# Layer 1's attention, two heads at a time: probabilities divided before they are turned, values as the stationary operand

## The chip, the cores and the metric

One core of a Trainium2 chip runs the whole program. The metric is device time in microseconds (us) of one execution, a median over runs; lower is better. A profile of one execution gives the start and the length of every instruction on the engines: TensorE (PE; its weight loads are listed as PEld), VectorE (DVE), ScalarE (ACT), GpSimd (POOL) and SyncE (SP), whose queue issues most DMAs.

## The reference, cut to what matters

A two-layer trunk over 256 frames of width 1024: retention and a dense feed-forward in layer 0, then shared keys and values, chunked attention and eight experts in layer 1. The change touches the attention alone. Each of 16 heads has 64 dimensions; a chunk of 64 frames attends to its own chunk and the eight before it, which with 256 frames means to all frames of its own and of earlier chunks.

```python
q = (xn @ w_q).reshape(B, nc, CHUNK, ATT_HEADS, ATT_HEAD_DIM) * (ATT_HEAD_DIM ** -0.5)
...
s = jnp.einsum('bihd,bjhd->bhij', q_c, k_band).astype(jnp.float32) + bias
s = jnp.where(valid, s, -jnp.inf)
a = jax.nn.softmax(s, axis=-1).astype(v_band.dtype)
return jnp.einsum('bhij,bjhd->bihd', a, v_band)
...
return o @ w_o
```

## The kernel before

Frames are two blocks of 128 (`tb` 0 and 1). Weights come from HBM as units of 1 MB through one queue (line 135, SP) into a few buffers; each unit is split into a high part (a cast on ScalarE, line 157) and the rest (a subtraction on VectorE, line 158), and a weight product is three matmuls with these parts. A buffer is free for the next load when its last subtraction is done.

Before the stage that the change touches, queries and keys are projected so that they lie turned: `qT` and `kT` hold 64 dimensions of the even head of a pair on partitions 0 to 63 and of the odd head on 64 to 127, with the 256 frames along the free axis. `vsb` holds the values with frames on the partitions. The first half of the heads is projected ahead of the loop. The second half's 8 rounds of 24 matmuls (lines 400 to 402, tile `kqps`) fill the first 8 rounds of the attention loop (`fill`). From the ninth round on the fill is the output projection, `out1(ch, tb)`: six matmuls of 512 columns each (lines 414, 415 and 418, tile `y`) for a chunk of 128 attended columns (two heads) and one block of frames.

A round `n` of the loop does, for one head each:

- `score(n)`: two f32 matmuls with 64 rows (lines 946 and 947, tile `sc`): the second block's queries against 256 keys, the first block's against 128. Then on VectorE the bias is added (950, 951), two maxima are taken (955, 956) and negated (957), and on ScalarE two exponentials (960, 963) also write the sums of their rows. After the odd head of a pair one reciprocal of four sums follows (967).
- `turn(n - 2)`: three transposes of 128 x 128 (974, tile `at`) and a copy out of PSUM on ScalarE (977).
- `values(n - 3)`: three f32 matmuls with the turned probabilities stationary, 128 columns, and 64 columns of values streaming (987 to 989, tile `ao`). After the odd head four scalings by the reciprocals write `dst` (996).
- `att_oT`, every second round: two transposes of a chunk of `dst` (1042, tile `otr`), split into high part and rest for the output projection (363, 364).

An f32 matmul of the program appears in the trace as two loads and two matmuls. In the loop the scheduler sets the order of every engine's work; after it an order written out by hand begins (`order`), which the last output chunks follow. PSUM has a ring of four banks (`bank`) for all of these tiles. The bias of a pair of heads is loaded by two DMAs (891, 892) into one of two buffers after the last add that reads the buffer.

The constants sit in one tile `cst` (loaded in two parts, lines 308 and 315); the exponent -0.5 of the norms, `nhalf`, has a tile of its own, set on line 316 and read on GpSimd.

Of the kernel before, what the change touches and what calls it, by code (L numbers as in the profile page):

```python
# [9 lines left out]
F32 = mybir.dt.float32  # L10
# [77 lines left out]
E_X, E_Y, E_END = 0, 8, 64  # L88
# [130 lines left out]
def trunk(ctx: ExitStack, tc: tile.TileContext, a, out):  # L219
# [15 lines left out]
    cst = base.tile([P, C_TILE], F32, name="cst")[:, :C_DEC]  # L235
    ext = base.tile([P, E_END], F32, name="ext")
    ones = base.tile([P, P], F32, name="ones")
    nhalf = base.tile([P, LINE], F32, name="nhalf")[:, :1]
# [642 lines left out]
    ap3 = r3.enter_context(tc.tile_pool(name="att3", bufs=3))  # L881
    vsb = ap_.tile([P, 2, D], F32, name="vsb")
# [54 lines left out]
    class Att:  # L937
# [3 lines left out]
        def score(self, hd):  # L941
            half, ch, par = hd // 8, (hd % 8) // 2, hd % 2
            rr = slice(par * 64, par * 64 + 64)
            q, k = qT[half][rr, ch, :], kT[half][rr, ch, :]
            b = bank("sc")
            nc.tensor.matmul(b[:, :T], q[:, P:], k, start=True, stop=True)
            nc.tensor.matmul(b[:, T : T + P], q[:, :P], k[:, :P], start=True, stop=True)
            bt = bias[(hd // 2) % 2][:, par, :]
            s = ap3.tile([P, T + P], F32, name="s")
            nc.vector.tensor_tensor(s[:, :T], b[:, :T], bt, op=OP.add)  # L950
            nc.vector.tensor_tensor(s[:, T:], b[:, T : T + P], bt[:, P:], op=OP.add)
            if par == 1 and hd // 2 + 2 < 8:
                load_bias(hd // 2 + 2)
            nm = s1("nm", 2)
            nc.vector.tensor_reduce(nm[:, 0:1], s[:, T:], axis=AX.X, op=OP.max)
            nc.vector.tensor_reduce(nm[:, 1:2], s[:, :T], axis=AX.X, op=OP.max)
            nc.vector.tensor_scalar(nm, nm, -1.0, None, op0=OP.mult)
            if par == 0:
                self.sum = s1("esum", 4)
            nc.scalar.activation(  # L960
                s[:, :T], s[:, :T], AF.Exp, bias=nm[:, 1:2], accum_out=self.sum[:, 2 + par : 3 + par]
            )
            nc.scalar.activation(s[:, T:], s[:, T:], AF.Exp, bias=nm[:, 0:1], accum_out=self.sum[:, par : par + 1])
            self.s[hd] = s
            if par == 1:
                rs = s1("rsum", 4)
                nc.vector.reciprocal(rs, self.sum)
                self.e[hd // 2] = rs
# [11 lines left out]
        def values(self, hd, dst):  # L980
            par = hd % 2
            t = self.t.pop(hd)
            if par == 0:
                self.o = bank("ao")
            o = self.o[:, :T].rearrange("p (b d) -> p b d", b=4)
            d = slice(hd * 64, hd * 64 + 64)
            nc.tensor.matmul(o[:, par, :], t[:, T:], vsb[:, 0, d], start=True, stop=True)
            nc.tensor.matmul(o[:, 2 + par, :], t[:, :P], vsb[:, 0, d], start=True, stop=False)
            nc.tensor.matmul(o[:, 2 + par, :], t[:, P:T], vsb[:, 1, d], start=False, stop=True)
            if par == 1:  # L990
                rs = self.e.pop(hd // 2)
                ch = (hd % 8) // 2
                for tb in range(2):
                    for j in range(2):
                        c = ch * P + j * 64
                        nc.vector.tensor_scalar(
                            dst[tb][:, c : c + 64], o[:, 2 * tb + j, :], rs[:, 2 * tb + j : 2 * tb + j + 1], None, op0=OP.mult
                        )
# [28 lines left out]
    dst, xo, wo, swapped, late = [], [], {}, [], []  # L1027
# [6 lines left out]

    def att_oT(ch):

        if ch % 2 == 0:
            xo.append(take_ht())
        b = bank("otr")[:, :T].rearrange("p (b t) -> p b t", b=2)
        c = ch % 4 * P  # L1040
        for tb in range(2):
            nc.tensor.transpose(b[:, tb, :], dst[ch // 4][tb][:, c : c + P], ident)
        f = slice(ch % 2 * 2, ch % 2 * 2 + 2)
        with hp(H1):
            split_bank(xo[-1][0][:, f, :], xo[-1][1][:, f, :], b)
# [14 lines left out]
    for n in range(19):  # L1060
        if n < 16:
            att.score(n)
        if n < 8:
            next(fill, None)
        if n == 8:
            for _ in fill:
                pass
            if not RE:
                st.retire(pairs1)
            elif not st.retired:  # L1070
                swap_right()
        for _ in range(PC if n % PM == 0 else 0):
            if late:
                st.raws.append(late.pop(0))
                st.load()
        if n >= 8 and n < 19 and outs[n - 8]:
            out1(*outs[n - 8])
        if 2 <= n <= 17:
            att.turn(n - 2)
        if n >= 3:  # L1080
            if (n - 3) % 8 == 0:
                dst.append([t512("ao0"), t512("ao1")])
            att.values(n - 3, dst[-1])
        if n >= 5 and n % 2:
            att_oT((n - 5) // 2)
    for x in OV[OO][1]:
        out1(*x)
    att_oT(7)
# [600 lines left out]
```

## Time and profile before

| | us |
|---|---|
| median of the runs shown | 1562.42 (1562.37 to 1562.57) |
| the profiled execution | 1563.2 |
| its span, first to last instruction | 1561.3 |
| busy: TensorE / weight loads / VectorE / ScalarE / GpSimd | 1537.8 / 1290.6 / 1275.3 / 1091.5 / 48.4 |

Busy time is the union of an engine's instructions. Matmuls overlap each other in flight: of two that follow each other, the first is still listed as running when the second starts. What a matmul costs TensorE is therefore the time from its start to the next one's start, not its listed length. The same holds, to a lesser degree, of VectorE and ScalarE. In a timeline neighbouring instructions of one kind are merged into a row (x2, x3), whose length runs from the first start to the last end.

### The profile page before, as it was taken

The numbers are of one execution on the slowest core, as the hardware profiler recorded it, in microseconds if no ns is written. First come the engines' busy times: TensorE is split into PE (matmuls) and PEld (weight loads), VectorE is DVE, ScalarE is ACT, GpSimd is POOL, SyncE is SP. The second block draws the span as 40 slices with busy tenths as digits, with TensorE's granted clock in tenths as the row PEclk, the third lists the DMA queues.
The fourth block names the chain that finished last, engine by engine and source line by source line (L and its number), as shares of the span: only waits on it lengthen the run. The fifth ranks groups of instructions, "written<-read, shape, count | busy, mean of one in ns | idle before, by whom it ended". The sixth has DMA issues, their size and how long they took to land.

```text
span 1561.3 us, 20789 instructions
## 1 busy us (share of the span) xinstructions
PE 1537.8 (98%) x7556; PEld 1290.6 (83%) x7556; DVE 1275.3 (82%) x1617; ACT 1091.5 (70%) x1461; POOL 48.4 (3%) x67
## 2 busy tenths in 40 slices
PE   7999999999999999999999999999999999999997
PEld 5888888888889888888888888888888888888886
DVE  7866675555774779999999999999999999999995
ACT  6545454554754658888878888888888788788774
POOL 1000010000000001000000000000000000000000
PEclk9999999999999999999999999999999999999999
DMA  8854476555463779999999999999999999999850
GB/s 294 286 180 167 162 254 216 187 188 196 149 217 124 267 269 378 412 391 381 378 382 394 381 373 388 366 382 390 373 386 391 375 368 398 380 369 390 310 211 30
DMA packets 206303, 473.56 MB, mean 303 GB/s; under 512 B 9168, under 2 KB 21328, under 8 KB 206192
## 3 DMA queue, kind: packets, MB, share of 16 engines
q1 hardware_dynamic: 202064, 457.87, 79.8%
q0 software_dynamic: 3840, 13.76, 2.4%
q8 instruction: 61, 1.00, 0.2%
q10 hardware_dynamic: 288, 0.52, 0.1%
q14 instruction: 50, 0.41, 0.1%
HBM read 462.16 MB, written 9.96 MB: 302 GB/s over the span
## 4 chain that ended last, share of the span: by engine, by line
PE 98%; ACT 1%; DVE 0%; DMA 0%; issue 0%; SPq 0%; POOL 0%; ACTq 0%; POOLq 0%; DVEq 0%
PE y L414 9%; PE y L415 9%; PE y L418 9%; PE g L333 8%; PE g L334 8%; PE g L335 8%; PE u L333 8%; PE u L335 8%; PE u L334 8%; PE vps L335 1%; PE vps L333 1%; PE vps L334 1%; PE htr L1230 1%; PE kqps L400 1%; PE qkps L401 1%; PE qkps L402 1%
## 5 line engine op out<-in xcount | busy, mean ns | idle before, releaser
L158 DVE TENSOR_TENSOR wlo<-raw,whi 128x512 fp32r<-128x512 f32 (+1 forms) x414 | 375.0, 929 | 109.5 <-ACT whi L157 94.4
L157 ACT CAST whi<-raw 128x512 fp32r<-128x512 f32 (+1 forms) x414 | 329.0, 812 | 139.0 <-PE y L418 49.7
L158 DVE TENSOR_TENSOR wlo<-more,whi 128x1024 fp32r<-128x1024 f32 (+1 forms) x275 | 327.4, 1214 | 26.4 <-ACT whi L157 14.1
L157 ACT CAST whi<-more 128x1024 fp32r<-128x1024 f32 (+1 forms) x275 | 284.6, 1049 | 58.6 <-PE y L418 29.5
L414 PE MATMUL y<-whi,ht 128*128 128x512 f32 x548 | 216.0, 394 | 0.5 <-ACT ht L363 0.5
L415 PE MATMUL y<-wlo,ht 128*128 128x512 f32 x548 | 213.9, 390 | 0.0
L333 PE MATMUL u<-whi,xd 128*128 128x512 f32 x448 | 180.3, 402 | 0.0
L333 PE MATMUL g<-whi,xd 128*128 128x512 f32 x456 | 177.9, 390 | 0.2 <-ACT xd L363 0.2
L335 PE MATMUL g<-whi,xd 128*128 128x512 f32 x456 | 177.9, 390 | 0.0
L334 PE MATMUL g<-wlo,xd 128*128 128x512 f32 x456 | 177.5, 389 | 0.0
L335 PE MATMUL u<-whi,xd 128*128 128x512 f32 x448 | 175.2, 391 | 0.0
L334 PE MATMUL u<-wlo,xd 128*128 128x512 f32 x448 | 174.5, 389 | 0.0
L418 PE MATMUL y<-whi,ht 128*128 128x512 f32 x548 | 169.0, 390 | 0.0
L414 PEld LDWEIGHTS y<-whi,ht 128*128 128x128 f32 x548 | 102.9, 188 | 21.9 <-ACT ht L363 1.0
L418 PEld LDWEIGHTS y<-whi,ht 128*128 128x128 f32 x548 | 102.9, 188 | 21.8
L415 PEld LDWEIGHTS y<-wlo,ht 128*128 128x128 f32 x548 | 103.0, 188 | 20.8
L158 DVE TENSOR_TENSOR wlo<-mraw,whi 128x1024 fp32r<-128x1024 f32 x91 | 109.3, 1223 | 10.3 <-ACT whi L157 5.1
L157 ACT CAST whi<-mraw 128x1024 fp32r<-128x1024 f32 x91 | 94.7, 1056 | 19.1 <-PE y L418 9.5
L158 DVE TENSOR_TENSOR wlo<-spare,whi 128x1024 fp32r<-128x1024 f32 x84 | 100.6, 1221 | 8.1 <-ACT whi L157 4.3
L335 PEld LDWEIGHTS g<-whi,xd 128*128 128x128 f32 x456 | 85.6, 188 | 18.2 <-DVE xd L364 0.4
L333 PEld LDWEIGHTS g<-whi,xd 128*128 128x128 f32 x456 | 85.6, 188 | 18.1 <-ACT xd L363 0.5
L157 ACT CAST whi<-spare 128x1024 fp32r<-128x1024 f32 x84 | 87.5, 1055 | 18.6 <-PE y L418 9.1
(363 smaller groups left out, 2632.0 us busy)
## 6 DMA issues: line engine op xcount, KB each, us to landing
more<-in_w_gate_moe_dram SPq DMA_DIRECT2D x56, 1024.0 KB, 7.1
more<-in_w_down_moe_dram SPq DMA_DIRECT2D x46, 1024.0 KB, 7.7
raw<-in_w_up_moe_dram SPq DMA_DIRECT2D x45, 1024.0 KB, 7.0
more<-in_w_up_moe_dram SPq DMA_DIRECT2D x35, 1024.0 KB, 7.0
raw<-in_w_gate_moe_dram SPq DMA_DIRECT2D x25, 1024.0 KB, 7.2
raw<-in_w_in_a_dram SPq DMA_DIRECT2D x23, 1024.0 KB, 5.2
raw<-in_w_down_moe_dram SPq DMA_DIRECT2D x22, 1024.0 KB, 7.3
mraw<-in_w_down_moe_dram SPq DMA_DIRECT2D x22, 1024.0 KB, 7.1
```

What stands on the lines that cost most here:

```text
L157: self.nc.scalar.copy(hi[:, f], r[:, g])
L158: (lo_engine or self.nc.vector).tensor_tensor(lo[:, f], r[:, g], hi[:, f].bitcast(F32), op=OP.subtract)
L333: nc.tensor.matmul(o, lh, rh, start=start, stop=False)
L334: nc.tensor.matmul(o, lh, rl, start=False, stop=False)
L335: nc.tensor.matmul(o, ll, rh, start=False, stop=stop)
L400: nc.tensor.matmul(o, wh[:, c, f], xh_, start=k == 0, stop=False)
L401: nc.tensor.matmul(o, wh[:, c, f], xl_, start=False, stop=False)
L402: nc.tensor.matmul(o, wl[:, c, f], xh_, start=False, stop=k == KC - 1)
L414: nc.tensor.matmul(ys[nb], xs[0][:, k, :], wh[:, c, f], start=first and k == 0, stop=False)
L415: nc.tensor.matmul(ys[nb], xs[0][:, k, :], wl[:, c, f], start=False, stop=False)
L418: nc.tensor.matmul(ys[nb], xs[1][:, k, :], wh[:, c, f], start=False, stop=last and k == n - 1)
L1230: nc.tensor.transpose(b[:, c, :m], x[:m, c0 + c * P : c0 + (c + 1) * P], ident[:m, :m])
```

## The change

Scores are computed for two heads at once, as four neighbouring matmuls: even and odd head for 256 keys, then both for 128. After the exponentials each head takes its own reciprocal of two sums, and two scalings divide the probabilities in place, ahead of the turn. `values(pr)` has the values of a head stationary (64 columns) and the turned probabilities streaming (256 columns, then 128). The even head's result lands on partitions 0 to 63 of a bank, the odd head's on 64 to 127, frames along the free axis. That is the turned chunk that the output projection reads, so `att_oT` goes: the bank is split at once. The layout of `s` is reversed (first block first). The loop runs over nine pairs of rounds instead of 19 rounds, and TensorE's order in it is the order in which it is written; `between(n)` is the projection or output round that was `fill` or `out1` before. `s` has four buffers of its own, and `nhalf` becomes a column of the constants' tile.

```diff
-E_X, E_Y, E_END = 0, 8, 64
+E_X, E_Y, E_END = 0, 8, 16
...
-    cst = base.tile([P, C_TILE], F32, name="cst")[:, :C_DEC]
+    cst_all = base.tile([P, C_TILE], F32, name="cst")
+    cst, nhalf = cst_all[:, :C_DEC], cst_all[:, C_DEC : C_DEC + 1]
...
-    nhalf = base.tile([P, LINE], F32, name="nhalf")[:, :1]
...
+    ap4 = r3.enter_context(tc.tile_pool(name="att4", bufs=4))
...
-        def score(self, hd):
...
+        def scores(self, pr):
+
+            half, ch = pr // 4, pr % 4
+            rows2 = [slice(par * 64, par * 64 + 64) for par in range(2)]
+            qk = [(qT[half][rr, ch, :], kT[half][rr, ch, :]) for rr in rows2]
+            bs = [bank("sc") for _ in range(2)]
+            for b, (q, k) in zip(bs, qk):
+                nc.tensor.matmul(b[:, P : P + T], q[:, P:], k, start=True, stop=True)
+            for b, (q, k) in zip(bs, qk):
+                nc.tensor.matmul(b[:, :P], q[:, :P], k[:, :P], start=True, stop=True)
+            for par in range(2):
+                self.exps(2 * pr + par, bs[par])
+
+        def exps(self, hd, b):
...
+            s = ap4.tile([P, T + P], F32, name="s")
...
+            sums = s1("esum", 2)
+            nc.scalar.activation(s[:, P:], s[:, P:], AF.Exp, bias=nm[:, 1:2], accum_out=sums[:, 1:2])
+            nc.scalar.activation(s[:, :P], s[:, :P], AF.Exp, bias=nm[:, 0:1], accum_out=sums[:, 0:1])
+            nc.vector.reciprocal(sums, sums)
+            nc.vector.tensor_scalar(s[:, P:], s[:, P:], sums[:, 1:2], None, op0=OP.mult)
+            nc.vector.tensor_scalar(s[:, :P], s[:, :P], sums[:, 0:1], None, op0=OP.mult)
             self.s[hd] = s
...
-        def values(self, hd, dst):
...
+        def values(self, pr):
+
+            b = bank("ao")
+            two = [(b[j * 64 : j * 64 + 64], self.t.pop(2 * pr + j), slice((2 * pr + j) * 64, (2 * pr + j) * 64 + 64)) for j in range(2)]
+            for o, t, d in two:
+                nc.tensor.matmul(o[:, :T], vsb[:, 0, d], t[:, :T], start=True, stop=False)
+            for o, t, d in two:
+                nc.tensor.matmul(o[:, P:T], vsb[:, 1, d], t[:, T:], start=False, stop=True)
+            if pr % 2 == 0:
+                xo.append(take_ht())
+            f = slice(pr % 2 * 2, pr % 2 * 2 + 2)
+            with hp(H1):
+                split_bank(xo[-1][0][:, f, :], xo[-1][1][:, f, :], b[:, :T].rearrange("p (b t) -> p b t", b=2))
...
-    def att_oT(ch):
...
+    by_pairs = tc.manual_schedule(engines={mybir.EngineType.PE})
+    by_pairs.__enter__()
+
+    def between(n):
         if n < 8:
             next(fill, None)
+        elif outs[n - 8]:
+            out1(*outs[n - 8])
+
+    for m in range(9):
+        if m < 8:
+            att.scores(m)
+        if m == 4:
             for _ in fill:
                 pass
...
+        if late:
+            st.raws.append(late.pop(0))
+            st.load()
+        between(2 * m)
+        if m:
+            att.turn(2 * m - 2)
+            att.turn(2 * m - 1)
+        between(2 * m + 1)
+        if m:
+            att.values(m - 1)
+    by_pairs.__exit__(None, None, None)
     for x in OV[OO][1]:
         out1(*x)
-    att_oT(7)
```

## Rows read from the trace of the kernel before

**Rows 1.** The page: busy time of the engines, and TensorE's tenths in 40 slices

```profile
PE 1537.8 (98%) x7556; PEld 1290.6 (83%) x7556; DVE 1275.3 (82%) x1617; ACT 1091.5 (70%) x1461; POOL 48.4 (3%) x67
...
PE   7999999999999999999999999999999999999997
```

**Rows 2.** Busy by stretch: PE, PEld, DVE, ACT, POOL; then granted clock, DMA share, GB/s

```profile
477.25:549.96 72.71, 72.26 (x483) 63.67 (x482) 44.60 (x152) 40.72 (x116) 0.00 (x0) 1.00 0.55 193
...
600.00:700.00 100.00, 100.00 (x465) 82.90 (x464) 93.30 (x95) 80.52 (x86) 3.19 (x4) 1.00 1.04 402
```

**Rows 3.** Waits of the load queue, 560 to 1540: total us, times, longest

```profile
SPq L135 <- DVE wlo L158: 776.5, 324, 12.0
```

**Rows 4.** Timeline (start, length) of TensorE at 459: projection steps

```profile
459.68 0.28 PE L401 MATMUL kqps<-xt,phi 128*128 128x256 f32 x1
459.80 0.28 PE L402 MATMUL kqps<-xt,plo 128*128 128x256 f32 x1
```

**Rows 5.** Timeline around the score block of head 8, TensorE and its weight loads

```profile
513.90 0.47 PE L414 MATMUL y<-whi,ht 128*128 128x512 f32 x1
514.30 0.70 PE L946 MATMUL sc<-kT,qT 64*128 64x256 f32 x2
514.62 0.40 PEld L947 LDWEIGHTS sc<-kT,qT 64*128 64x128 f32 x2
514.84 0.38 PE L947 MATMUL sc<-kT,qT 64*128 64x128 f32 x2
515.15 0.50 PE L415 MATMUL y<-wlo,ht 128*128 128x512 f32 x1
515.49 0.40 PE L414 MATMUL y<-whi,ht 128*128 128x512 f32 x1
...
516.43 0.49 PE L974 MATMUL at<-cst,s 128*128 128x128 f32 x3
516.76 0.33 PE L987 MATMUL ao<-vsb,at 128*128 128x64 f32 x2
```

**Rows 6.** Groups by line, 477.25 to 549.96: busy us, mean ns, idle before

```profile
L158 DVE TENSOR_TENSOR wlo<-raw,whi 128x512 fp32r<-128x512 f32 x24 | 15.8, 687 | 3.8 <-ACT whi L157 3.8
...
L996 DVE TENSOR_SCALAR ao<-ao,rsum 128x64 f32<-128x64 f32 x32 | 7.2, 278 | 10.3 <-PE ao L989 10.3
...
L364 DVE TENSOR_TENSOR ht<-otr,ht 128x256 fp32r<-128x256 f32 x8 | 3.4, 421 | 3.4 <-ACT ht L363 3.3
...
L363 ACT CAST ht<-otr 128x256 fp32r<-128x256 f32 x8 | 3.0, 374 | 2.9 <-PE otr L1042 2.9
```

**Rows 7.** One line's instructions: a scaling of 256 columns, min/median/max ns

```profile
L476 DVE TENSOR_SCALAR ang<-ang,cst x1: 354/354/354, 23.5 to 23.5; 128x256 f32<-128x256 f32 x1
```

**Rows 8.** Timelines of VectorE and ScalarE, 524.8 to 527.5: one head's chain

```profile
524.80 0.16 DVE L957 TENSOR_SCALAR nm<-nm 128x2 f32<-128x2 f32 x1
...
525.73 0.42 DVE L950 TENSOR_TENSOR s<-sc,bias 128x256 f32<-128x256 f32 x1 [0.20 <-PE sc L947]
...
526.60 0.28 DVE L955 TENSOR_REDUCE nm<-s 128x1 f32<-128x128 f32 x1
...
525.00 0.51 ACT L960 ACTIVATE s<-s,nm 128x256 f32<-128x256 f32 x1 [0.48 <-DVE nm L957]
...
525.80 0.19 ACT L963 ACTIVATION_READ_ACCUMULATOR s<-s,nm 128x1 f32 x1
527.47 0.48 ACT L977 COPY at<-at 128x384 f32<-128x384 f32 x1 [1.49 <-PE at L974]
```

**Rows 9.** DMA issues from 476 to 550: count, KB each, median us to landing

```profile
bias<-in_bias_hi_dram SPq DMA_DIRECT2D x6, 128.0 KB, 3.1
```

**Rows 10.** The constants' tile, 0 to 24: its readers, its loads, their time to landing

```profile
L369 PE MATMUL xtr<-cst,xh x16: 421/421/476, 10.1 to 17.9; 128*128 128x128 f32 x16
...
L315 SPq DMA_DIRECT2D cst<-in_cst_dram x1: 1098/1098/1098, 4.1 to 4.1; - x1
...
DMA to landing us min/median/max: 1.9/5.5/9.2
```

More of the change, by code (lines that the diff above doesn't have):

```diff
@@ L939, in __init__ @@
             self.s, self.e, self.t = {}, {}, {}
-        def score(self, hd):
[L942 to L947, printed above, removed]
+        def scores(self, pr):
[10 more added lines that the diff above has]
+        def exps(self, hd, b):
+            par = hd % 2
             bt = bias[(hd // 2) % 2][:, par, :]
-            s = ap3.tile([P, T + P], F32, name="s")
-            nc.vector.tensor_tensor(s[:, :T], b[:, :T], bt, op=OP.add)
-            nc.vector.tensor_tensor(s[:, T:], b[:, T : T + P], bt[:, P:], op=OP.add)
+            s = ap4.tile([P, T + P], F32, name="s")
+            nc.vector.tensor_tensor(s[:, P:], b[:, P : P + T], bt, op=OP.add)
+            nc.vector.tensor_tensor(s[:, :P], b[:, :P], bt[:, P:], op=OP.add)
             if par == 1 and hd // 2 + 2 < 8:
@@ L954, in score @@
             nm = s1("nm", 2)
-            nc.vector.tensor_reduce(nm[:, 0:1], s[:, T:], axis=AX.X, op=OP.max)
-            nc.vector.tensor_reduce(nm[:, 1:2], s[:, :T], axis=AX.X, op=OP.max)
+            nc.vector.tensor_reduce(nm[:, 0:1], s[:, :P], axis=AX.X, op=OP.max)
+            nc.vector.tensor_reduce(nm[:, 1:2], s[:, P:], axis=AX.X, op=OP.max)
             nc.vector.tensor_scalar(nm, nm, -1.0, None, op0=OP.mult)
[L958 to L963, printed above, removed]
+            sums = s1("esum", 2)
[4 more added lines that the diff above has]
+            nc.vector.tensor_scalar(s[:, :P], s[:, :P], sums[:, 0:1], None, op0=OP.mult)
             self.s[hd] = s
[L965 to L968, printed above, removed]
         def turn(self, hd):
@@ L978, in turn @@
             self.t[hd] = t
-        def values(self, hd, dst):
[L981 to L998, printed above, removed]
+        def values(self, pr):
[10 more added lines that the diff above has]
+                split_bank(xo[-1][0][:, f, :], xo[-1][1][:, f, :], b[:, :T].rearrange("p (b t) -> p b t", b=2))
     att = Att()
@@ L1026, in trunk @@
     y = new_y()
-    dst, xo, wo, swapped, late = [], [], {}, [], []
+    xo, wo, swapped, late = [], {}, [], []
     def swap_right():
@@ L1033, in swap_right @@
         swapped.append(True)
-    def att_oT(ch):
[L1037 to L1045, printed above, removed]
     def out1(ch, tb, n=99):
@@ L1059, in trunk @@
     outs = [(0, 0), (0, 1), (1, 0), (1, 1), (2, 0), (2, 1), (3, 0), (3, 1)] + OV[OO][0]
-    for n in range(19):
-        if n < 16:
-            att.score(n)
+    by_pairs = tc.manual_schedule(engines={mybir.EngineType.PE})
+    by_pairs.__enter__()
+    def between(n):
         if n < 8:
             next(fill, None)
-        if n == 8:
+        elif outs[n - 8]:
[4 more added lines that the diff above has]
+        if m == 4:
             for _ in fill:
                 pass
-            if not RE:
-                st.retire(pairs1)
-            elif not st.retired:
+            if not st.retired:
                 swap_right()
[L1072 to L1085, printed above, removed]
+        if late:
[9 more added lines that the diff above has]
+    by_pairs.__exit__(None, None, None)
     for x in OV[OO][1]:
         out1(*x)
-    att_oT(7)
     order = tc.manual_schedule(engines=eng)
```

## The prediction, made before the result was known

> **What bounds the kernel now.** I read the page's busy line and its slices first: TensorE is busy 98% of the span, and no slice but the first and the last is under 9 tenths [rows 1]. That alone proves little, since the ends of matmuls are modelled; so I looked at the stretch that the change touches, from the first score matmul to the first output matmul of the last chunk, 477.25 to 549.96, 72.7 us. There TensorE is covered for 72.26 us at a granted clock of 1.00 (the 2.4 GHz level), VectorE for 44.60 and ScalarE for 40.72 [rows 2]; the 0.45 us left open is the wait for the last turned chunk. So in this stage the time is the sum of the steps from one matmul's start to the next one's, and the change is worth the difference of two such sums. The other engines matter only if they come to keep TensorE waiting.
>
> Is a gain kept afterwards? In the experts TensorE is covered 100.00 of 100 us [rows 2], while the queue of weight loads waits for free buffers (776.5 us in 324 waits from 560 to 1540) [rows 3]. TensorE sets the pace there too, and the loads are ahead of it. A stage that ends 10 us earlier starts the experts 10 us earlier; I keep the whole gain.
>
> **The parts of the stage.** What stays: 192 projection matmuls of 256 columns (eight rounds of 24) at 0.12 us from start to start [rows 4], 23.0 us; 66 output matmuls of 512 columns (eleven rounds of six) at 0.235 (four steps from 515.49 to 516.43 [rows 5]), 15.5 us; 48 turns at 0.109 (0.33 for three [rows 5]), 5.2 us. Together 43.7 us. The other 72.7 - 43.7 = 29.0 us are scores, values, 16 transposes of attended rows, and the edges between kinds of work.
>
> One score block shows the edges [rows 5]. The output matmul ahead of it starts at 513.90 and the block at 514.30: 0.40 where 0.235 is usual, so 0.17 is a wait for the array to empty. The second pass starts with the load at 514.62 and takes until 514.84, 0.215; the first took 0.32, so 0.107 of it is a weight load that nothing hides. The four passes (each f32 matmul is two) are 2 x 0.215 + 2 x 0.108 = 0.645; the block ends at 515.15, 0.85 after its start, so 0.094 more is a wait behind it. The matmul after that takes 0.34: another 0.107 of unhidden load. Entering a 64-row block costs 0.28, leaving it 0.20.
>
> **Scores.** Two heads now stand side by side, one on partitions 0 to 63, one on 64 to 127. Nothing in the trace has two neighbouring matmuls on opposite halves, so I bound it. One after the other, a pair is 2 x 0.645 = 1.29; wholly side by side it is 0.645. The two passes of a head share their rows and must follow each other, and the order is A, A, B, B, then the shorter A, A, B, B, started in order. Then A's second pass runs beside B's first, B's second beside the short A's first, and so on: 0.215 x 3 + 0.108 x 2 = 0.86. I take that, an estimate between the ends: only the order stands in the way, not the rows.
>
> **Values.** Now 64 columns of values stand still, and 256, then 128, columns of turned probabilities stream. That is as many columns as in the scores, so the prices of a pair are the same: 0.86, between 0.645 and 1.29. (Before, the six passes of a head were followed after some 0.6 to 0.7 us.) The new blocks get edges that the old ones, 128 wide, did not have; I price them as the score block's.
>
> **Edges.** In the written order there are 10 entries from 128-wide work (two scores, eight values), 10 exits to it, and 6 places where values are followed at once by scores: 10 x 0.28 + 10 x 0.20 + 6 x 0.20 = 6.0 us.
>
> **Transposes of attended rows** are gone, 16 x 0.11 = 1.8 us, with the 0.45 us wait at the end: the last values are now followed by a whole round of output (1.4 us), which hides one cast and one subtraction (0.37 and 0.42 [rows 6]).
>
> **Sum.** 29.0 us becomes 8 x 0.86 + 8 x 0.86 + 6.0 = 19.8, a gain of 9.2. With everything wholly side by side it is 12.7, with everything one after the other 2.4.
>
> **VectorE and ScalarE.** Out go 32 scalings (0.278 us [rows 6]) and 8 reciprocals; in come 16 reciprocals and 32 larger scalings, for which the nearest row is 0.354 us (256 columns, a scalar per partition) [rows 7]. That is some 3 us more VectorE work, beside 28 us of slack [rows 2]: nothing on the path. But it lies in the chain from scores to turns. For a pair: adds and maxima 1.15 us a head and a negation 0.16, twice, 2.6; exponentials of the second head 1.0; reciprocal and two scalings 0.8; some 4.5 us with the hand-overs [rows 7, 8]. Its cover in the second half of the loop is three output rounds (4.2), two turns (0.65), a values and a score block (2.4): 7.2 us. Two subtractions of weights and one of a chunk (0.69, 0.69, 0.42 [rows 6]) may stand between: 6.3. It fits, barely.
>
> Less sure is the copy of turned probabilities. It had a whole head's round until its use; now it has one output round, 1.4 us, in the second half. Two copies of 0.48 fit, but the next pair's exponentials (1.0 a head) come to ScalarE at the same time [rows 8]. Behind none of them the values wait 0, behind one head's 0.75 us: over the four such rounds 0 to 3.0 us, and nothing in the first half, where a round is 2.9 us. I take 1.2. What is queued behind such a wait is all of TensorE's work, since its order is now written out.
>
> The moved bias loads (two DMAs a pair, 3.1 us to land [rows 9]) are issued after the second head's adds and wanted two rounds, over 12 us, later: nothing, and 3 us a round if they stood behind a blocked weight load in their queue. The norms' constant moves into the tile of the large constants, whose second load, issued at 4.1, takes up to 9.2 to land; the transposes at 10.1 already read that tile's first columns before then [rows 10], so columns are told apart: nothing, or some 5 us at the start if they were not.
>
> The Trainium skill, "TensorEngine Tiling (Array Packing)", section "Key Properties", says that changing the tiling mode drains TensorE; that speaks against this change, which makes a second tiled block of the values. The rows' 0.17 and 0.094 bear a drain out for rows; none shows one for columns. Were the values free of it, the edges would be those of eight score blocks, 8 x 0.48 = 3.8 us, and the gain 11.4; by the rule it stays 9.2.
>
> **Rivals.** (a) *Nothing runs side by side.* Only edges and transposes are saved: 2.4 less 1.2 of waiting, 1561.2 us. For it: no row shows two matmuls streaming at once. Against it: a score matmul uses 64 rows and costs what its columns cost, so the other half is idle. (b) *Only scores overlap,* or only values: 9.2 - 8 x 0.43 - 1.2 = 4.6, 1557.8. (c) *Slower: each change of half is an edge.* A block of a pair changes halves three times, 48 times in 16 blocks. At the 0.20 of leaving and reloading that is 9.6 us on top of (a), 1570.8 us; the loss passes 3.1 us from 4.3 / 48 = 0.09 us a change. For it: the trace has no change without other work between. Against it: within a block a load runs ahead during the pass before it. (d) *Slower: the divided probabilities come late,* and the written order holds all of TensorE for them. Past 7.2 us of chain each us is paid in five rounds; at 9.7 it is 12.5 us against 9.2, 1565.7. For it: 6.3 of 7.2 are used. (e) *Wholly side by side:* 12.7 less 1.2, 1550.9. Against it: a head's two passes share their rows.
>
> Of (e), the Trainium skill, "TensorE: Matmul & The Clock Gate", section "Measured speedup vs the span model", says that a packed group lasts about one matmul plus 4 ns a tile. By it the time would be that of (e); no run here shows it, and it does not speak of two-pass f32 matmuls.
>
> **How the numbers follow.** The profiled execution took 1563.2 us (span 1561.3); less 9.2, plus 1.2, that is 1555.2. The median of the runs shown, 1562.42, is 0.8 lower, so I forecast 1554.4. Chances: forecast 0.60, (a) 0.13, (b) 0.11, (c) 0.06, (d) 0.05, (e) 0.05. The range, 1549.7 (12.7 gained, no waiting) to 1563.0 (2.4 gained, 3.0 of waits), leaves out (c) and (d). A difference under 0.2%, 3.1 us, can't be told from none: faster is the forecast, (b) and (e), nearly all of it, 0.75; same is most of (a), 0.14; slower 0.11.
>
> **What would show it.** Right: score passes of opposite halves that start under 0.1 us apart; a pair's score block and values block near 1.06 us each with the first load and the wait behind; under 2 us of waits of TensorE in the stage; a stage near 65 us. Wrong: blocks of 1.5 us (a), gaps at each change of half (c), TensorE waiting for VectorE ahead of turns (d), or for the copies by more than 3 us. A later stage that gives the gain back would upset the second paragraph.

## The result, and the profile after

| us | before | after |
|---|---|---|
| median of the runs compared | 1562.49 (1562.37 to 1562.90) | 1549.49 (1549.08 to 1549.70) |
| the profiled execution, and its span | 1563.2, 1561.3 | 1549.7, 1547.9 |
| the stage, first score matmul to first output matmul of the last chunk | 72.68 | 59.40 |
| the rest, from there to the end of the span | 1011.37 | 1011.28 |

After takes 0.9917 of the time of before (95% interval 0.9905 to 0.9929): 13.0 us faster. The forecast was 1554.4, and the range ended 0.2 us above the measured time, at 1549.7. That miss is smaller than the spread of after's own runs (0.6 us); the distance to the forecast, 4.9 us, is not, and it is what has to be explained. The stage shrank by 13.28 us, and what follows took as long as ever (1011.07 to 1011.45 in every kernel below). The stage begins between 476.0 and 477.6 us, up to 1.6 us apart in these kernels, so below the length of the stage says more than the median.

The page and the windows of after, to lay beside [rows 1, 2]: TensorE is still the engine that is hardly ever idle, also in the stage.

```profile
PE 1524.8 (99%) x7508; PEld 1276.6 (82%) x7508; DVE 1277.0 (82%) x1625; ACT 1090.1 (70%) x1461; POOL 48.2 (3%) x67
...
PE   7999999999999999999999999999999999999997
```
```profile
477.24:536.64 59.40, 59.24 (x435) 49.81 (x435) 46.95 (x160) 39.24 (x116) 0.00 (x0) 1.00 0.61 216
...
600.00:700.00 100.00, 100.00 (x465) 82.94 (x464) 93.01 (x96) 81.06 (x89) 1.60 (x3) 1.00 1.03 398
```

Within the stage TensorE is covered 59.24 of 59.40 us, VectorE 46.95, ScalarE 39.24. The waits of the load queue from 560 to 1540 are those of [rows 3], one fewer:

```profile
SPq L135 <- DVE wlo L158: 775.8, 323, 11.9
```

Now the blocks. The timeline of TensorE in after, around the scores of pair 5 (start, length, merged rows), to lay beside [rows 5]:

```profile
514.24 0.70 PE L949 MATMUL sc<-kT,qT 64*128 64x256 f32 x4
514.77 0.39 PE L951 MATMUL sc<-kT,qT 64*128 64x128 f32 x4
515.09 0.50 PE L414 MATMUL y<-whi,ht 128*128 128x512 f32 x1
```

The first row lasts 0.70 us, as that of [rows 5] did, but holds four passes, not two. The block ends 0.85 after its start, as one head's did. Two heads cost what one did. That the passes of the two heads start together, a narrow stretch shows (514.05 to 514.245; the x2 are one pass of each head):

```profile
513.81 0.49 PE L993 MATMUL ao<-at,vsb 128*64 128x128 f32 x3
514.24 0.49 PE L949 MATMUL sc<-kT,qT 64*128 64x256 f32 x2
```

In the single records they start at 514.236 and 514.242, 0.006 us apart, and the other three couples of the block by 0.007. Pairs are counted from 0, and the round that computes the scores of pair 5 ends with the values of pair 4. These, in the same view:

```profile
518.25 0.62 PE L418 MATMUL y<-whi,ht 128*128 128x512 f32 x2
518.79 0.65 PE L991 MATMUL ao<-at,vsb 128*64 128x256 f32 x4
519.28 0.39 PE L993 MATMUL ao<-at,vsb 128*64 128x128 f32 x4
519.60 0.49 PE L949 MATMUL sc<-kT,qT 64*128 64x256 f32 x2
```

Eight passes in 0.80 us (518.79 to 519.60). Over the stage all eight score blocks take 0.85, seven of the eight values blocks 0.80 and one 1.01.

The groups by line of after in the stage, to lay beside [rows 6, 7]:

```profile
L158 DVE TENSOR_TENSOR wlo<-raw,whi 128x512 fp32r<-128x512 f32 x24 | 15.6, 683 | 1.2 <-ACT whi L157 1.1
...
L972 DVE TENSOR_SCALAR s<-s,esum 128x256 f32<-128x256 f32 x16 | 5.6, 351 | 0.4
...
L973 DVE TENSOR_SCALAR s<-s,esum 128x128 f32<-128x128 f32 x16 | 4.5, 280 | 0.0
...
L364 DVE TENSOR_TENSOR ht<-ao,ht 128x256 fp32r<-128x256 f32 x8 | 3.4, 419 | 7.7 <-ACT ht L363 7.7
```

### The profile page after: what moved, and what is told of

Its sections match the earlier page's. It is cut to its first block, busy times and chain, and to the rows that moved or that the text cites. A ratio compares the mean times of both kernels' runs of the same rounds, so it can differ in the third digit from the quotient of the medians.

```text
span 1547.9 us, 20705 instructions
## 1 busy us (share of the span) xinstructions
PE 1524.8 (99%) x7508; PEld 1276.6 (82%) x7508; DVE 1277.0 (82%) x1625; ACT 1090.1 (70%) x1461; POOL 48.2 (3%) x67
## 4 chain that ended last, share of the span: by engine, by line
PE 98%; DVE 0%; ACT 0%; DMA 0%; issue 0%; SPq 0%; POOL 0%; ACTq 0%; POOLq 0%; DVEq 0%
PE y L414 9%; PE y L415 9%; PE y L418 9%; PE g L333 8%; PE g L335 8%; PE g L334 8%; PE u L333 8%; PE u L335 8%; PE u L334 8%; PE vps L335 1%; PE vps L333 1%; PE vps L334 1%; PE htr L1219 1%; PE kqps L400 1%; PE qkps L402 1%; PE qkps L401 1%
## 5 line engine op out<-in xcount | busy, mean ns | idle before, releaser
L158 DVE TENSOR_TENSOR wlo<-mraw,whi 128x1024 fp32r<-128x1024 f32 x91 | 109.3, 1222 | 10.3 <-ACT whi L157 5.2
```

The costliest lines, as they stand in the source:

```text
L158: (lo_engine or self.nc.vector).tensor_tensor(lo[:, f], r[:, g], hi[:, f].bitcast(F32), op=OP.subtract)
```

## The experiments

Every kernel is the changed kernel with one edit. The table gives, in us, the median with its range, the ratio to the kernel before on the same chip with its 95% interval, and from the profiled execution the stage, and the time from the start of a score block and of a values block to the next work's start, as it is in most of the eight rounds.

| | median | ratio to before | stage | scores | values |
|---|---|---|---|---|---|
| after | 1549.49 (1549.08 to 1549.70) | 0.9917 [0.9905, 0.9929] | 59.40 | 0.85 | 0.80 |
| scores_one_half | 1554.31 (1553.91 to 1554.40) | 0.9946 [0.9929, 0.9962] | 64.10 | 1.50 | 0.80 |
| values_one_half | 1554.90 (1554.34 to 1555.36) | 0.9951 [0.9935, 0.9968] | 64.42 | 0.85 | 1.44 |
| head_after_head | 1548.99 (1547.96 to 1549.36) | 0.9910 [0.9894, 0.9927] | 59.13 | 0.86 | 0.81 |
| even_head_thrice | 1559.85 (1559.22 to 1560.35) | 0.9982 [0.9972, 0.9991] | 69.91 | 2.26 | 0.80 |
| even_short_four | 1556.66 (1555.72 to 1556.98) | 0.9959 [0.9944, 0.9974] | 66.65 | 1.83 | 0.80 |
| scores_apart | 1557.07 (1556.59 to 1557.28) | 0.9964 [0.9950, 0.9978] | 66.91 | 0.85 a head | 0.80 |
| old_values | 1553.66 (1553.38 to 1554.13) | 0.9943 [0.9927, 0.9960] | 64.02 | 0.85 | 1.38 and, in two, 1.26 |
| no_division | 1549.51 (1549.37 to 1549.72) | 0.9917 [0.9900, 0.9933] | 59.02 | 0.85 | 0.80 |
| turns_late | 1557.88 (1556.74 to 1558.64) | 0.9968 [0.9956, 0.9980] | 67.09 | 0.85 | 1.18 |
| scheduled_order | 1548.56 (1547.92 to 1549.32) | 0.9910 [0.9894, 0.9927] | 58.90 | 0.85 | 0.80 |
| split_first | 1549.18 (1548.85 to 1549.70) | 0.9914 [0.9900, 0.9927] | 59.38 | 0.85 | 0.80 |
| scheduled_split_first | 1548.34 (1547.78 to 1549.63) | 0.9906 [0.9891, 0.9922] | 58.92 | 0.85 | 0.80 |

### Is it the halves? scores_one_half and values_one_half

Both heads' scores from the same rows; then both heads' values onto the same partitions (written head after head, and with the split in two parts, from two column ranges of the bank).

```diff
-            rows2 = [slice(par * 64, par * 64 + 64) for par in range(2)]
+            rows2 = [slice(0, 64) for par in range(2)]
```
```diff
-            two = [(b[j * 64 : j * 64 + 64], ...
+            two = [(b[:64, j * T : j * T + T], ...
             for o, t, d in two:
                 nc.tensor.matmul(o[:, :T], vsb[:, 0, d], t[:, :T], start=True, stop=False)
-            for o, t, d in two:
                 nc.tensor.matmul(o[:, P:T], vsb[:, 1, d], t[:, T:], start=False, stop=True)
...
```

> The changed kernel with both heads' scores taken from partitions 0 to 63 (the odd head's scores are the even head's; that part of the result is not computed). Theory S: in the changed kernel the score passes of the two heads run wholly side by side, a block of a pair lasts one head's 0.645 us plus edges. Then one half must do both heads' passes in turn: a score block grows from 0.85 to 1.50 us, 8 x 0.645 = 5.2 us in all, about 1554.7 us. Rival E: the gain is in fewer edges and in the written order, overlap does nothing; then 1549.5, blocks unchanged.

> The changed kernel with both heads' values written to partitions 0 to 63 of the bank, the odd head's to its own columns, and split from there in two parts (8 more casts and 8 more subtractions of 64 partitions, off TensorE). Theory S: a values block grows from 0.80 to 1.45 us, 5.2 us in all, about 1554.7 us, up to 1 us more if the additional casts come to hold a PSUM bank. Rival E: 1549.5.

The timeline of TensorE in scores_one_half, one pair's scores:

```profile
517.42 1.13 PE L949 MATMUL sc<-kT,qT 64*128 64x256 f32 x4
518.38 0.60 PE L951 MATMUL sc<-kT,qT 64*128 64x128 f32 x4
518.92 0.50 PE L414 MATMUL y<-whi,ht 128*128 128x512 f32 x1
```

The same eight passes on the same rows take 1.50 instead of 0.85, and the stage 4.70 us more; the values on the same partitions take 1.44 instead of 0.80, and the stage 5.02 more. Eight times 0.645 is 5.2; the first kernel also lost some 0.5 us of the waits that after has. The order head after head in the second is not what it pays for: on two halves that order costs next to nothing (head_after_head, below). So rows side by side and columns side by side are each worth a whole block of passes a pair: the theory that the halves run wholly side by side holds for both.

### Does the written order limit it? head_after_head

The prediction took 0.86 for the passes, not 0.645, on the premise that matmuls start in the order in which they are written. If they do, the order even 256, even 128, odd 256, odd 128 must be slower still.

```diff
                 nc.tensor.matmul(b[:, P : P + T], q[:, P:], k, start=True, stop=True)
-            for b, (q, k) in zip(bs, qk):
                 nc.tensor.matmul(b[:, :P], q[:, :P], k[:, :P], start=True, stop=True)
```

(and the same in `values`)

> The changed kernel with the four matmuls of a block written head after head (even 256, even 128, odd 256, odd 128 columns; the values alike). Theory I: each half of the array takes its own matmuls as they come, whatever stands between them in the order; then the blocks keep 0.85 and 0.80 us and the time stays 1549.5. Rival Q (the prediction's step): matmuls start in the order in which they are written, so only the even head's last short pass meets the odd head's first: a block grows by 0.645 - 0.108 = 0.54 us, 16 blocks by 8.6 us, 1558.1.

Its timeline of TensorE, one pair's scores:

```profile
519.63 0.71 PE L949 MATMUL sc<-kT,qT 64*128 64x256 f32 x4
520.17 0.40 PE L950 MATMUL sc<-kT,qT 64*128 64x128 f32 x4
520.49 0.50 PE L414 MATMUL y<-whi,ht 128*128 128x512 f32 x1
```

The four passes of line 949 still share 0.71 us: the odd head's first pass starts beside the even head's first, although two shorter passes of the even head are written ahead of it. A block takes 0.86, the stage 59.13 (blocks 0.007 longer than in after, waits 0.4 us less in sum). The order within a block costs next to nothing, and the prediction's step falls.

### How far ahead does a half start? even_head_thrice and even_short_four

To find the end of that freedom, the even head's two matmuls stand three times ahead of the odd head's; then, to part a count of passes from a length of time, its short matmul four times.

```diff
-            for b, (q, k) in zip(bs, qk):
+            for b, (q, k) in [(bs[0], qk[0])] * 2 + list(zip(bs, qk)):
                 nc.tensor.matmul(b[:, P : P + T], q[:, P:], k, start=True, stop=True)
-            for b, (q, k) in zip(bs, qk):
                 nc.tensor.matmul(b[:, :P], q[:, :P], k[:, :P], start=True, stop=True)
```
```diff
-            for b, (q, k) in zip(bs, qk):
+            for j, (b, (q, k)) in enumerate(zip(bs, qk)):
                 nc.tensor.matmul(b[:, P : P + T], q[:, P:], k, start=True, stop=True)
-            for b, (q, k) in zip(bs, qk):
-                nc.tensor.matmul(b[:, :P], q[:, :P], k[:, :P], start=True, stop=True)
+                for _ in range(4 if j == 0 else 1):
+                    nc.tensor.matmul(b[:, :P], q[:, :P], k[:, :P], start=True, stop=True)
```

> The changed kernel with the even head's two score matmuls issued three times, head after head, then the odd head's once: twelve passes of the even half stand ahead of the odd half's four. Theory I without limit: the odd head's first pass starts within 0.02 us of the even head's first, the block lasts three heads' passes, 1.94 us plus edges (2.14), 8 x 1.29 = 10.3 us more, 1559.8. Rival Q: the odd head starts after the even head's last pass but one, block 2.67 us, 14.6 us more, 1564.1. Theory L (independent, but only as far ahead as the queue looks): the odd head's first pass starts between, and its delay shows how many passes the halves may drift apart.

> The changed kernel with head after head in the scores and the even head's matmul of 128 columns issued four times: ten passes of the even half, 2 of 256 and 8 of 128 columns, stand ahead of the odd half's four. With the even head's pair of matmuls issued three times the odd half started beside the ninth of twelve even passes, three passes still to come. Theory P, a lead of so many passes: the odd half starts beside the seventh of ten, 0.107 + 2 x 0.215 + 4 x 0.108 = 0.97 us after the even half, the block ends 0.645 later and is 1.7 us long with the wait behind. Theory T, a lead of so much streaming (0.43 us after the ninth began, four short passes): it starts beside the sixth, 0.86 after. Without a limit: beside the first, block 1.50.

The timeline of TensorE in even_head_thrice, one pair's scores:

```profile
484.70 0.70 PE L949 MATMUL sc<-kT,qT 64*128 64x256 f32 x2
485.24 0.38 PE L950 MATMUL sc<-kT,qT 64*128 64x128 f32 x2
485.46 0.59 PE L949 MATMUL sc<-kT,qT 64*128 64x256 f32 x2
485.89 0.38 PE L950 MATMUL sc<-kT,qT 64*128 64x128 f32 x2
486.11 0.70 PE L949 MATMUL sc<-kT,qT 64*128 64x256 f32 x4
486.55 0.49 PE L950 MATMUL sc<-kT,qT 64*128 64x128 f32 x4
```

The first four rows are the even head alone; only in the fifth, at 486.11, does the odd head appear. In the single records its first pass starts 0.006 after the even head's ninth of twelve, with three still to come, in each of the eight blocks. The block takes 2.26: twice 0.645, the unhidden first load of 0.107, and a last round of 0.85 side by side. The time, 1559.85, happens to be the 1559.8 that free halves would have given, for which the block should have been 2.14; the start of the odd head decides, not that number.

In even_short_four:

```profile
483.78 0.70 PE L949 MATMUL sc<-kT,qT 64*128 64x256 f32 x2
484.31 0.72 PE L951 MATMUL sc<-kT,qT 64*128 64x128 f32 x5
484.76 0.48 PE L949 MATMUL sc<-kT,qT 64*128 64x256 f32 x1
```

The odd head's first pass (third row) comes 0.006 after the even head's seventh of ten (the fifth of the x5): three still to come again, though these three are short ones, where in even_head_thrice one long and two short were left. So of the two theories the lead is counted in passes, not in streaming time. head_after_head fits, with three passes still to come at the start, but can't show the limit, since the odd head has nothing to wait for there. The block takes 1.83, not the 1.7 of that theory, because the theory left out a load: the odd head's first pass takes 0.320 (484.762 to 485.082), 0.107 of it a load that nothing hides, as at the start of every block. From its start to the next work the odd head needs 0.85 (484.762 to 485.608), what one head alone needs, and 0.99 + 0.85 is 1.83. What in the hardware makes it three passes, these runs don't say.

### What does an edge cost? scores_apart

The odd head's scores stand after the following round, so that each head's block is alone again. This adds eight blocks with an entry and an exit each.

```diff
+                self.exps(2 * pr + par, b)
+                yield
...
-        if m < 8:
-            att.scores(m)
+        sc = att.scores(m) if m < 8 else iter(())
+        next(sc, None)
...
         between(2 * m)
+        next(sc, None)
```

> The changed kernel with the odd head's scores moved behind the round of projection or output that follows, so that the two heads' scores are never neighbours. Theory S: per pair 0.645 us of passes that no longer run beside others, and one more entry (0.28) and exit (0.20): 8 x 1.13 = 9.0 us, 1558.5. Rival O: only overlap counts and edges cost nothing, 5.2 us, 1554.7.

The timeline of TensorE: an entry from output work, and a block of one head:

```profile
514.85 0.62 PE L418 MATMUL y<-whi,ht 128*128 128x512 f32 x2
515.39 0.70 PE L949 MATMUL sc<-kT,qT 64*128 64x256 f32 x2
515.93 0.38 PE L950 MATMUL sc<-kT,qT 64*128 64x128 f32 x2
516.24 0.88 PE L979 MATMUL at<-cst,s 128*128 128x128 f32 x6
```

One head alone takes 0.85 (515.39 to 516.24), as a pair does. The stage grew by 7.5 us, where 9.0 was expected with the prediction's entry of 0.28. The last output matmul starts at 515.076 and the block at 515.395: 0.32, so the wait to empty is 0.088, not 0.17, and an entry costs 0.088 + 0.107 = 0.195. With that, 8 x (0.645 + 0.195 + 0.20) = 8.3, less some 0.5 us of waits that after has and this kernel hasn't: 7.8. The last 0.3 us is the exit: in seven of eight rounds the added block is followed by the turns, and there the first turn takes 0.165 (516.242 to 516.407) where 0.109 is usual, so 0.056 of load shows and not 0.107. Seven times 0.05 us is 0.35.

### Scores or values? old_values

The values again with turned probabilities stationary, and the attended rows transposed back; the pairs of scores, the division and the written order stay.

```diff
...
+                nc.tensor.matmul(o[:, par, :], t[:, :P], vsb[:, 0, d], start=True, stop=True)
+                nc.tensor.matmul(o[:, 2 + par, :], t[:, P:T], vsb[:, 0, d], start=True, stop=False)
+                nc.tensor.matmul(o[:, 2 + par, :], t[:, T:], vsb[:, 1, d], start=False, stop=True)
...
+            nc.tensor.transpose(b[:, tb, :], dst[ch // 4][tb][:, c : c + P], ident)
```

> The changed kernel with the values computed as before (turned probabilities stationary, 64 columns streaming, two copies of 128 columns to rows of attended frames, two transposes and a split per pair); scores stay side by side, division ahead of the turn and the written order stay. Theory S, from the blocks of the changed kernel's trace: a values block with its entry is 0.10 + 0.80 = 0.90 us; the old way is 1.25 for twelve passes, 0.22 for two transposes and 0.09 of entry into the next scores, 1.56; 8 x 0.66 = 5.3 us and some 0.5 at the end, 1555.3 us. Rival V: all of the gain lies in the scores, the values' new edges eat what their side by side brings; then 1549.5 to 1551.

The stage is 64.02: 4.6 us more than after's, 8.7 less than before's. The values of a pair take 1.38 in six rounds and 1.26 in two, 1.35 on average, and the transposes 0.22: 1.57 against 0.80 and an entry's wait of 0.09 in after. Eight times 0.68 is 5.4, and the 0.8 us of waits that after has are gone (0.03 is left), which makes the 4.6. So of the 13.3 us about a third came with the new values and the transposes that they spare, and about two thirds with the rest, the pairing of the scores above all: the division and the written order, which old_values has too, change the stage by half a us or less (no_division and scheduled_order, below).

### The division: no_division

The reciprocal and the two scalings left out.

> The changed kernel without the reciprocals and the scalings (the probabilities are not divided, the result lacks the softmax's sums). The changed kernel's trace has two waits of 0.27 us between the two turns of a round. Theory B: they wait for a bank of PSUM that the split of the values frees late; VectorE has 3 us less to do, so these waits may shrink, but nothing else does: 1549.0 to 1549.5. Rival D: the divided probabilities are late in every round of the second half; then 1548 or less and no wait is left ahead of the turns.

The stage is 0.38 us shorter, the median the same (1549.51). In its trace the waits of after between the two turns (twice 0.27, once 0.07) are gone, and a second values block waits 0.21. The 16 reciprocals and 32 scalings on VectorE are therefore worth at most 0.4 us, by what they delay behind them: all but off the path, as the prediction had it.

### The cover of the copies: turns_late

Both turns right ahead of the values, behind both rounds between, so that nothing lies between a turn's copy and its use.

```diff
         between(2 * m)
+        between(2 * m + 1)
...
             att.turn(2 * m - 1)
-        between(2 * m + 1)
-        if m:
             att.values(m - 1)
```

> The changed kernel with both turns moved behind the second round of projection or output, right ahead of the values: the copies of the turned probabilities lose their cover. Theory C: each values block waits for a copy of 0.48 us begun 0.25 after its turn, the odd head's a second 0.48 later: 0.5 to 1.0 us a pair, 4 to 8 us in all, 1553.5 to 1557.5. Rival: the copies were no matter even without cover, 1549.5.

The waits in its stage, 476.48 to 543.57 (engine and line, waited for: us in total, times, longest):

```profile
PEld ao L991 <- ACT at L983: 8.5, 16, 1.3
PE ao L991 <- ACT at L983: 4.6, 8, 1.1
```

The stage grew by 7.7 us, about 1 us a pair, the upper end of Theory C, and the waits say for what: the values' loads wait for the copies on ScalarE. In after no such wait is listed, and one of its eight values blocks waits 0.21 us: the odd head's load (513.440) comes 0.05 after a copy's end (513.389). The output or projection round between turns and values is a cover that is needed, and but for this one block it is enough.

### The written order, and the last waits: scheduled_order, split_first, scheduled_split_first

In after the second turn of a pair waited 0.27 us in two rounds. The timeline of one of them, in after:

```profile
521.35 0.68 DVE L158 TENSOR_TENSOR wlo<-raw,whi 128x512 fp32r<-128x512 f32 x1
...
521.95 1.08 PE L980 MATMUL at<-cst,s 128*128 128x128 f32 x6
521.95 0.42 DVE L364 TENSOR_TENSOR ht<-ao,ht 128x256 fp32r<-128x256 f32 x1
...
522.48 0.31 PEld L980 LDWEIGHTS at<-cst,s 128*128 128x128 f32 x3 [0.28 <-PE at L980]
```

The six turns take 1.08 us where 0.82 is usual, and the load of the fourth waits until 522.48, 0.11 after the split of the values (line 364) has ended. The split stood behind a subtraction of weights (line 158). My reading was that the second turn waits for the PSUM bank that the split reads. split_first gives the split a higher priority; scheduled_order lets the scheduler order TensorE's work in the loop; the last kernel does both.

```diff
-            with hp(H1):
+            with hp(60):
```
```diff
-    by_pairs = tc.manual_schedule(engines={mybir.EngineType.PE})
-    by_pairs.__enter__()
...
-    by_pairs.__exit__(None, None, None)
```

> The changed kernel with the split of the values' bank given a high priority, so that its subtraction on VectorE no longer stands behind subtractions of weights. Theory B: the two waits of 0.27 us between the turns of a round end when that bank comes free; they go, the stage falls from 59.4 to some 58.9 us, 1549.0 us. Rival D: they end when the odd head's probabilities are divided; then the stage stays at 59.4, or grows, since the adds and scalings now stand behind the split.

> The changed kernel without the order written out for TensorE in the loop: the scheduler sets it. Theory W: the scheduler starts what is ready first and pulls matmuls of other kinds between the two heads' passes, as it put score blocks into output rounds before; each pair that is torn costs 0.645 and an entry and exit, 1.13 us: 1551 to 1559 depending on how many are torn. Rival N: neighbours in the program stay neighbours; 1549.5, within 0.5.

> The changed kernel without the order written out for TensorE in the loop, and with the split of the values' bank first: both edits that took some tenths off the stage. If they add, the stage is 58.6 to 58.9 us and the time about 1548.7 us; below 58.8 us the sum of the parts without any wait (43.7 of unchanged work, 10.3 of passes, 4.8 of edges) leaves nothing to gain.

With the split earlier both waits are gone, which bears the reading out; but in the last round a new one appears, as the timeline of split_first shows:

```profile
531.13 0.49 PE L980 MATMUL at<-cst,s 128*128 128x128 f32 x3
531.94 0.52 PE L980 MATMUL at<-cst,s 128*128 128x128 f32 x3 [0.32 <-DVE s L973]
```

There the second turn waits for the odd head's division, since the split now goes ahead of it on VectorE. The stage stays at 59.38: 0.5 us was taken and 0.5 given back. With the scheduler's order the pairs of matmuls stay together (0.85 and 0.80, rival N), so the written order isn't where the gain comes from; the two turns part around output matmuls in two rounds, and the stage is 0.5 us shorter. The two edits together do not add up: 58.92, where 58.6 to 58.9 was expected and scheduled_order alone has 58.90. The last kernel has the lowest median, 1548.34, but its runs overlap those of after. What is left in waits is under 1 us, and no kernel here shows more to be had.

## Why the prediction was wrong, step by step

**The bound, and that the gain is kept: right.** TensorE's steps make up the stage before and after, and the rest took 1011.28 us against 1011.37.

**What stays, 43.7 us: right.** With it, 16 x 0.645 = 10.3 for passes, 4.8 for edges and 0.8 for waits (below) the stage comes to 59.6, against 59.40.

**The price of a pair: wrong, the largest term.** The prediction took 0.86 on the ground that "only the order stands in the way", and the order does not stand in the way: the other half's first pass starts beside the first one. The pair costs its lower bound, 0.645, for scores and for values (scores_one_half, values_one_half, head_after_head). 16 x 0.215 = 3.4 us. Rival (e), wholly side by side, was given 0.05 on the argument that a head's two passes share their rows. That is true, and beside the point: each head's passes follow each other, but the other head's follow theirs at the same time. Rival (e) is what happened, with edges 1.2 us and waits 0.4 us (both below) smaller than it took: 1550.9 less 1.6 is 1549.3. The Trainium skill, "TensorE: Matmul & The Clock Gate", section "Measured speedup vs the span model", had it right: its rule of one matmul plus some 4 ns for each further tile agrees with the 0.006 us between the starts, for two-pass f32 matmuls too, and with a block of 0.853 us for two heads where one head's takes 0.847.

**The edges: mis-sized.** An entry was read off one step of 0.40 in [rows 5]. The output matmul of that step stands right behind the transposes of attended rows; TensorE's timeline of before, just ahead of those rows:

```profile
513.76 0.39 PE L1042 MATMUL otr<-cst,ao 128*128 128x128 f32 x2
513.90 0.47 PE L414 MATMUL y<-whi,ht 128*128 128x512 f32 x1
```

In the single records it starts 0.027 us after the second transpose, which by its usual step takes 0.11: its start stands some 0.085 early, and the step behind it is as much too long. (Whether it is only listed early, the trace can't tell.) In after the same shows behind every pair of turns. Its timeline there:

```profile
511.08 0.82 PE L980 MATMUL at<-cst,s 128*128 128x128 f32 x6
511.65 0.48 PE L414 MATMUL y<-whi,ht 128*128 128x512 f32 x1
511.97 0.40 PE L415 MATMUL y<-wlo,ht 128*128 128x512 f32 x1
512.20 0.40 PE L414 MATMUL y<-whi,ht 128*128 128x512 f32 x1
```

Six turns take 0.57 to the next start, where 6 x 0.109 is 0.65, and the step behind is 0.32, where the next is 0.23: the two errors cancel in a sum, but not in a price read from one of the two steps. The trace of before held the right price too, at its entries from projections, which no short matmul precedes. Its timeline of TensorE at the first score block:

```profile
477.08 0.28 PE L402 MATMUL kqps<-xt,wlo 128*128 128x256 f32 x1
477.29 0.70 PE L946 MATMUL sc<-kT,qT 64*128 64x256 f32 x2
```

The step is 0.209 where 0.120 is usual, a wait of 0.089. An entry to scores costs 0.195 (scores_apart). One to values costs less: from the last output matmul at 518.469 to the block at 518.795 it is 0.326, a wait of 0.096, and the first pass takes 0.268, so the unhidden load of 64 columns is 0.053; together 0.15. Leaving was right: a wait of 0.094 behind a block's last pass and 0.107 of load in the next one's first, 0.20. From values to scores it is the same: the step from 514.034 to 514.236 is 0.202, of which the pass itself takes 0.109, and 0.107 of load follows. So the edges come to 2 x 0.195 + 8 x 0.15 + 10 x 0.20 + 6 x 0.20 = 4.8 us, not 6.0. This is why the time fell below even the range's low end, which had everything side by side but edges of 6.0.

**That values would pay an edge: right.** Their blocks have a wait on entering (0.096) that the old ones had not; without it the stage would be shorter still. The rule of the Trainium skill, "TensorEngine Tiling (Array Packing)", section "Key Properties", that a change of the tiling mode drains TensorE, agrees with this for columns as for rows.

**Waits, 1.2 us for copies: too many.** After's waits sum to some 0.8 us: 0.21 in the values block of 1.01, twice 0.27 and once 0.07 between turns. The copies account for at most the first (turns_late, above). The next pair's exponentials do not come at the same time as the copies, as was feared: the timeline of after, ScalarE and VectorE behind the turns of pair 4:

```profile
517.17 0.88 ACT L983 COPY at<-at 128x384 f32<-128x384 f32 x2 [1.57 <-PE at L980]
...
517.78 0.15 DVE L967 TENSOR_SCALAR nm<-nm 128x2 f32<-128x2 f32 x1
...
517.97 0.51 ACT L969 ACTIVATE s<-s,nm 128x256 f32<-128x256 f32 x1
```

ScalarE does both copies at once, because the exponentials wait for the negated maxima (517.78), and VectorE comes to these only after the division of the pair before. That the cover was needed turns_late shows. The two waits of 0.27, for a bank, were not foreseen.

**VectorE: right.** 46.95 us busy against 44.60, 2.4 more where 3 was said, and at most 0.4 us of it on the path (no_division). The scaling of 256 columns takes 351 ns, where 354 was taken from [rows 7].

**The edits with no price: right.** The bias lands 3.5 us after its issue, where [rows 9] had 3.1, and even the last load is there 2.4 us before the add that reads it (523.7 against 526.1). The stage starts at 477.24, as it did before (477.29), so the 5 us that the moved constant might have cost were not paid.

Together: 8.0 us were forecast; 3.4 for the passes, 1.2 for the edges and 0.4 for the waits make it 13.0, against 13.28 in the stage and 13.0 in the medians. Of the signs that the prediction named, the start of opposite passes under 0.1 us apart and waits under 2 us came true; the blocks of 1.06 and the stage near 65 did not.

## What to carry to other kernels

Matmuls that use half of TensorE's rows or columns should stand beside a neighbour on the other half: here the second one was free, in f32 with its two passes as well, whatever the order inside the block, even with four passes of its neighbour written ahead of it; with ten or twelve ahead it started late. Count the changes between such blocks and full-width work as edges of 0.15 to 0.20 us, and leave a round of other work between a producer on another engine and TensorE's use of it. Read the price of an edge from several places, and never from a step next to very short matmuls.

## What the runs showed of the hardware that was not expected

- Matmuls on opposite halves do not start in written order. In head_after_head the odd head's first pass starts beside the even head's first, ahead of the even head's shorter matmul. The Trainium skill, "TensorE: Matmul & The Clock Gate", section "The mechanism", has matmuls start and end strictly in order; these traces disagree on the starts (the ends are modelled). They list starts, not the stream of instructions: that the stream keeps the order written out in the kernel is taken from the kernel. In after's one disturbed values block it shows without any edit (the timeline of TensorE; the even head starts, the odd head waits for 0.2 us):

```profile
513.22 0.65 PE L991 MATMUL ao<-at,vsb 128*64 128x256 f32 x3
513.71 0.27 PE L993 MATMUL ao<-at,vsb 128*64 128x128 f32 x1
513.71 0.38 PE L991 MATMUL ao<-at,vsb 128*64 128x256 f32 x1
```

  Here the even head's shorter matmul (513.705) starts before the odd head's second pass over 256 columns (513.709), which is written ahead of it.
- The lead is limited: in two kernels the other half started only when three passes of the first were still to come, whether these were long or short (0.006 us after the ninth of twelve and the seventh of ten, in all blocks). In head_after_head it started 0.013 us after the first of four, where three were to come from the outset.
- At a granted clock of 1.00 a change from full-width work to 64 rows or 64 columns costs 0.088 to 0.096 us of waiting and an unhidden load of 0.107 or 0.053 us, and one from columns to rows, or back to full width, 0.20 (0.15 into the transposes of scores_apart).
